# RWKV time mixing on one core: one batch a tile with contiguous runs, a fixed software pipeline, and transposes of bf16 pairs as float32 words

## The chip, the core and the metric

The kernel runs on one core of one Trainium2 chip. The metric is the device time of one execution in microseconds (us), taken as the median of several runs. A profile shows one execution, engine by engine: PE (TensorE, matmuls; its weight loads stand apart as PEld), DVE (VectorE), ACT (ScalarE), POOL (GpSimd) and SP (SyncE, which here only issues DMAs).

## What is computed

The input `x` holds 16 batches of 2048 tokens with 256 channels, in float32. Each token is mixed with the token before it in its batch (zeros ahead of the first), two projections follow, one passes a sigmoid, and their product goes through an output projection. The reference also computes `k`, which nothing uses; neither kernel computes it.

```python
x_prev[:, 1:, :] = x[:, :-1, :]
xv = x * time_mix_v + x_prev * (1 - time_mix_v)
xr = x * time_mix_r + x_prev * (1 - time_mix_r)
v = xv @ value_weight
r = xr @ receptance_weight
out = (sigmoid(r) * v) @ output_weight
```

## The kernel before

The work goes in 32 tiles of 1024 tokens (two a batch), and each tile in two halves of 512 tokens. Both kernels divide the mixing weight out: with c = 1/t - 1, the mixed value is t * (x + c * x_prev), and t is multiplied into the rows of the projection's weights once, at the start. So a mix is one multiplication (`x_prev` by c) and one addition.

For each tile POOL issues one DMA that loads 1024 rows of 1 KB and casts them to bf16 (L102, `x_bf`, 4 buffers). PE transposes it in 16 blocks of 128 x 128 bf16 into PSUM (L114), so that channels lie on the partitions, in two groups of 128 channels (`ko`), and tokens along the free dimension. ACT copies the two PSUM tiles into `xt` (L120, L121), one column to the right, so that column t holds token t - 1; column 0 is a memset or a copy of the last tile's last column (L124, L126). DVE makes `mix`: four multiplications of 128 x 1024 (L132) and two additions of 128 x 2048 (L141), one for v and one for r. For each half PE makes `psum_v` and `psum_r` (L151, L160, four matmuls of 512 columns each), ACT takes the sigmoid of `psum_r` into `s_sb` (L169), DVE multiplies it by `psum_v` into `z_sb` (L171), PE makes `psum_o` with eight matmuls of 256 columns whose stationary operand is `z_sb` (L176), and ACT copies it to `o_sb` in bf16 (L183). After both halves POOL issues one DMA that stores the tile and casts it to float32 (L185).

`psum_v`, `psum_r` and `psum_o` have one buffer each. The order on each engine is made by the scheduler of the Tile framework; within an engine instructions run in that order. All DMAs of `x` and `out` stand in the one queue of POOL.

Of the kernel before, what the change touches and what calls it, by code (L numbers as in the profile page):

```python
# [1 line left out]

# [6 lines left out]
FP32 = mybir.dt.float32  # L10
BF16 = mybir.dt.bfloat16
ALU = mybir.AluOpType
ACT = mybir.ActivationFunctionType


@with_exitstack
def kernel(
    ctx: ExitStack,
    tc: tile.TileContext,
    x: bass.AP,  # L20
    time_mix_k: bass.AP,
    time_mix_v: bass.AP,
    time_mix_r: bass.AP,
    key_weight: bass.AP,
    value_weight: bass.AP,
    receptance_weight: bass.AP,
    output_weight: bass.AP,
    out: bass.AP,
):
# [12 lines left out]

    ident = consts.tile([P, P], BF16)
    make_identity(nc, ident)

    tmv_sb = consts.tile([P, KO], FP32)
    nc.sync.dma_start(out=tmv_sb, in_=time_mix_v.rearrange("(ko p) -> p ko", p=P))
    tmr_sb = consts.tile([P, KO], FP32)
    nc.sync.dma_start(out=tmr_sb, in_=time_mix_r.rearrange("(ko p) -> p ko", p=P))

    cv_sb = consts.tile([P, KO], FP32)
    nc.vector.reciprocal(cv_sb, tmv_sb)
    nc.vector.tensor_scalar(  # L53
        out=cv_sb, in0=cv_sb, scalar1=-1.0, scalar2=None, op0=ALU.add
    )
    cr_sb = consts.tile([P, KO], FP32)
    nc.vector.reciprocal(cr_sb, tmr_sb)
    nc.vector.tensor_scalar(
        out=cr_sb, in0=cr_sb, scalar1=-1.0, scalar2=None, op0=ALU.add
    )  # L60
    c_sb = [cv_sb, cr_sb]

    ones = consts.tile([P, T], BF16)
    nc.vector.memset(ones, 1.0)
    c_full = []
    for m in range(2):
        cf = consts.tile([P, KO, T], BF16, name=f"c_full{m}")
        for ko in range(KO):
            nc.scalar.mul(out=cf[:, ko, :], in_=ones, mul=c_sb[m][:, ko : ko + 1])  # L69
        c_full.append(cf)  # L70

    wv_f32 = consts.tile([P, KO, D], FP32)
    nc.sync.dma_start(out=wv_f32, in_=value_weight.rearrange("(ko p) n -> p ko n", p=P))
    wr_f32 = consts.tile([P, KO, D], FP32)
    nc.sync.dma_start(
        out=wr_f32, in_=receptance_weight.rearrange("(ko p) n -> p ko n", p=P)
    )

    wv_bf = consts.tile([P, KO, D], BF16)
    wr_bf = consts.tile([P, KO, D], BF16)  # L80
    wo_bf = consts.tile([P, KO, D], BF16)
    for ko in range(KO):
        nc.scalar.mul(out=wv_bf[:, ko, :], in_=wv_f32[:, ko, :], mul=tmv_sb[:, ko : ko + 1])
        nc.scalar.mul(out=wr_bf[:, ko, :], in_=wr_f32[:, ko, :], mul=tmr_sb[:, ko : ko + 1])
    nc.gpsimd.dma_start(out=wo_bf, in_=output_weight.rearrange("(ko p) n -> p ko n", p=P))  # L85

    xpool = ctx.enter_context(tc.tile_pool(name="xpool", bufs=4))
    xtpool = ctx.enter_context(tc.tile_pool(name="xtpool", bufs=3))
    mixpool = ctx.enter_context(tc.tile_pool(name="mixpool", bufs=3))
    zpool = ctx.enter_context(tc.tile_pool(name="zpool", bufs=4))  # L90
    opool = ctx.enter_context(tc.tile_pool(name="opool", bufs=3))
    ps_xt_pool = ctx.enter_context(tc.tile_pool(name="ps_xt", bufs=2, space=bass.MemoryType.PSUM))
    ps_vr_pool = ctx.enter_context(tc.tile_pool(name="ps_vr", bufs=1, space=bass.MemoryType.PSUM))
    ps_o_pool = ctx.enter_context(tc.tile_pool(name="ps_o", bufs=1, space=bass.MemoryType.PSUM))

    prev_xt = None
    for b in range(B):
        for it in range(NT):
            t0 = it * T

            x_bf = xpool.tile([P, 2 * HB, D], BF16, name="x_bf")
            nc.gpsimd.dma_start(  # L102
                out=x_bf,
                in_=x[b, t0 : t0 + T, :].rearrange("(tb p) d -> p tb d", p=P),
            )

            xt = xtpool.tile([P, KO, XTW], BF16, name="xt")

            psum_xt = []
            for h in range(2):  # L110
                ps = ps_xt_pool.tile([P, KO, TH], BF16, name="ps_xt")
                for tb in range(HB):
                    for ko in range(KO):
                        nc.tensor.transpose(  # L114
                            out=ps[:, ko, tb * P : (tb + 1) * P],
                            in_=x_bf[:, h * HB + tb, ko * P : (ko + 1) * P],
                            identity=ident,
                        )
                psum_xt.append(ps)
            nc.scalar.copy(out=xt[:, :, 1 : 1 + TH], in_=psum_xt[0])  # L120
            nc.scalar.copy(out=xt[:, :, 1 + TH : 1 + T], in_=psum_xt[1])  # L121

            if it == 0:
                nc.vector.memset(xt[:, :, 0:1], 0.0)  # L124
            else:
                nc.vector.tensor_copy(out=xt[:, :, 0:1], in_=prev_xt[:, :, T : T + 1])  # L126
            prev_xt = xt

            mix = mixpool.tile([P, 2, KO, T], BF16, name="mix")
            for m in range(2):  # L130
                for ko in range(KO):
                    nc.vector.tensor_scalar(  # L132
                        out=mix[:, m, ko, :],
                        in0=xt[:, ko, 0:T],
                        scalar1=c_sb[m][:, ko : ko + 1],
                        scalar2=None,
                        op0=ALU.mult,
                    )
            xwin = xt[:, :, 1 : T + 1]
            for m in range(2):  # L140
                nc.vector.tensor_tensor(  # L141
                    out=mix[:, m], in0=mix[:, m], in1=xwin, op=ALU.add
                )

            o_sb = opool.tile([P, 2, HB, D], BF16, name="o_sb")
            for h in range(2):
                psum_v = ps_vr_pool.tile([P, KO, TH], FP32, name="psum_v")
                psum_r = ps_vr_pool.tile([P, KO, TH], FP32, name="psum_r")
                for mo in range(KO):
                    for ko in range(KO):  # L150
                        nc.tensor.matmul(  # L151
                            out=psum_v[:, mo, :],
                            lhsT=wv_bf[:, ko, mo * P : (mo + 1) * P],
                            rhs=mix[:, 0, ko, h * TH : (h + 1) * TH],
                            start=(ko == 0),
                            stop=(ko == KO - 1),
                        )
                for mo in range(KO):
                    for ko in range(KO):
                        nc.tensor.matmul(  # L160
                            out=psum_r[:, mo, :],
                            lhsT=wr_bf[:, ko, mo * P : (mo + 1) * P],
                            rhs=mix[:, 1, ko, h * TH : (h + 1) * TH],
                            start=(ko == 0),
                            stop=(ko == KO - 1),
                        )

                s_sb = zpool.tile([P, KO, TH], BF16, name="s_sb")
                nc.scalar.activation(out=s_sb, in_=psum_r, func=ACT.Sigmoid)  # L169
                z_sb = zpool.tile([P, KO, TH], BF16, name="z_sb")  # L170
                nc.vector.tensor_tensor(out=z_sb, in0=s_sb, in1=psum_v, op=ALU.mult)  # L171

                psum_o = ps_o_pool.tile([P, HB, D], FP32, name="psum_o")
                for j in range(HB):
                    for ko in range(KO):
                        nc.tensor.matmul(  # L176
                            out=psum_o[:, j, :],
                            lhsT=z_sb[:, ko, j :: HB],
                            rhs=wo_bf[:, ko, :],
                            start=(ko == 0),  # L180
                            stop=(ko == KO - 1),
                        )
                nc.scalar.copy(out=o_sb[:, h], in_=psum_o)  # L183

            nc.gpsimd.dma_start(  # L185
                out=out[b, t0 : t0 + T, :].rearrange("(h p j) d -> p h j d", p=P, j=HB),
                in_=o_sb,
            )


# [28 lines left out]
```

## Time and profile before

| what | value |
|---|---|
| median of 3 runs | 261.02 us (259.26 to 261.79) |
| span of the profiled execution | 258.6 us |
| PE busy | 208.8 us, 81% of the span |
| DVE busy | 205.3 us, 79% |
| ACT busy | 192.0 us, 74% |
| POOL busy | 53.0 us, 20% |
| HBM read and written | 34.34 MB and 33.55 MB |

The span runs from the first to the last instruction of the profiled execution. A line of a group gives the source line, the engine, the operation, output and inputs by name, the shape and the count, then busy time and the mean of one in ns, then the idle time of the engine just before these instructions and what ended it. A line of the timeline gives start and duration in us, then the same names; a merged line has the count behind an x, and idle time and its releaser in brackets. Durations of neighbours on one engine overlap by some tens of ns, so what an instruction costs its engine is read from start to start.

### The profile page before, as it was taken

What the parts mean: (1) busy time and instruction counts of PE and PEld (TensorE: products, weight loads), DVE (VectorE), ACT (ScalarE), POOL (GpSimd) and SP (SyncE); (2) the same over time, 40 slices, a digit from 0 to 9 for tenths busy, and PEclk for the clock granted to TensorE, in tenths of its full rate; (3) what the DMA queues carried; (4) which work ended last, traced back from release to release, by engine and by line L of the source; (5) the groups of instructions that cost most, each with busy time, mean ns of one, the idle gap of its engine ahead of it and who ended that gap; (6) DMA issues with size and microseconds to landing.
All of it is one profiled execution on the core that took longest, in us unless ns stands there. A gap on an engine that the chain in (4) does not pass through costs nothing.

```text
span 258.6 us, 3915 instructions
## 1 busy us (share of the span) xinstructions
PE 208.8 (81%) x1508; PEld 136.5 (53%) x1536; DVE 205.3 (79%) x293; ACT 192.0 (74%) x202; POOL 53.0 (20%) x71
## 2 busy tenths in 40 slices
PE   0288989888988889888889888988888987787860
PEld 0265655555666556565556655655555664354430
DVE  3087999888889888888888998888888899885330
ACT  6678979777777887877777788787777777645640
POOL 7031421222222211222222221112211111100111
PEclk9999999999999999999999999999999999999997
DMA  5999999999999999999999999999974343344444
GB/s 114 188 198 197 150 270 220 275 230 233 227 202 200 197 214 245 238 219 231 228 230 213 197 195 206 243 243 224 224 205 162 111 153 119 116 153 165 162 162 162
DMA packets 43362, 51.24 MB, mean 198 GB/s; under 512 B 1616, under 2 KB 35152, under 8 KB 43344
## 3 DMA queue, kind: packets, MB, share of 16 engines
q0 software_dynamic: 42256, 50.47, 89.3%
q1 hardware_dynamic: 1088, 0.53, 0.7%
q8 instruction: 12, 0.20, 0.3%
q14 instruction: 6, 0.05, 0.1%
HBM read 34.34 MB, written 33.55 MB: 263 GB/s over the span
## 4 chain that ended last, share of the span: by engine, by line
issue 67%; POOL 16%; PE 6%; DMA 4%; ACT 3%; POOLq 1%
POOL x_bf L102 8%; POOL out_dram L185 8%; DMA x_bf<-in_x_dram 4%; PE ps_xt L114 2%; PE psum_v L151 2%; PE psum_r L160 1%; PE psum_o L176 1%; ACT xt L120 1%; ACT s_sb L169 1%; ACT xt L121 1%; POOL wo_bf L85 0%; ACT o_sb L183 0%; POOLq L214 0%; POOLq L185 0%; POOLq L102 0%
## 5 line engine op out<-in xcount | busy, mean ns | idle before, releaser
L171 DVE TENSOR_TENSOR z_sb<-s_sb,psum_v 128x1024 bf16<-128x1024 bf16 x64 | 77.8, 1216 | 31.6 <-PE psum_v L151 28.3
L183 ACT CAST o_sb<-psum_o 128x1024 bf16<-128x1024 f32 x64 | 65.9, 1030 | 37.3 <-PE psum_o L176 37.3
L176 PE MATMUL psum_o<-wo_bf,z_sb 128*128 128x256 bf16 x512 | 67.3, 274 | 16.5 <-DVE z_sb L171 16.4
L169 ACT ACTIVATE s_sb<-psum_r 128x1024 bf16<-128x1024 f32 x64 | 66.0, 1032 | 17.5 <-PE psum_r L160 16.6
L141 DVE TENSOR_TENSOR mix<-mix,xt 128x2048 bf16<-128x2048 bf16 x64 | 77.7, 1218 | 0.0
L160 PE MATMUL psum_r<-mix,wr_bf 128*128 128x512 bf16 x244 | 65.2, 379 | 5.1 <-ACT s_sb L169 4.4
L176 PEld LDWEIGHTS <-z_sb 128*128 128x128 bf16 x512 | 52.1, 115 | 30.8 <-DVE z_sb L171 30.5
L151 PE MATMUL psum_v<-mix,wv_bf 128*128 128x512 bf16 x240 | 64.3, 382 | 0.7 <-issue 0.2
L114 PE MATMUL ps_xt<-ident,x_bf 128*128 128x128 bf16 x512 | 41.0, 228 | 20.5 <-DMA x_bf<-in_x_dram 12.0
L185 POOL DMA_DIRECT2D out_dram<-o_sb x32 | 22.6, 705 | 169.2 <-ACT o_sb L183 169.2
L114 PEld LDWEIGHTS <-x_bf 128*128 128x128 bf16 x512 | 35.6, 102 | 37.8 <-issue 15.4
L160 PEld LDWEIGHTS <-wr_bf 128*128 128x128 bf16 x256 | 25.1, 98 | 30.1 <-issue 0.7
L132 DVE TENSOR_SCALAR mix<-xt,cv_sb 128x1024 bf16<-128x1024 bf16 x64 | 28.7, 490 | 9.4 <-ACT xt L121 9.3
L120 ACT COPY xt<-ps_xt 128x1024 bf16<-128x1024 bf16 x32 | 32.7, 1021 | 3.7 <-PE ps_xt L114 3.7
L102 POOL DMA_DIRECT2D x_bf<-in_x_dram x32 | 29.0, 907 | 30.5 <-PE ps_xt L114 30.4
L151 PEld LDWEIGHTS <-wv_bf 128*128 128x128 bf16 x256 | 25.2, 99 | 16.1 <-issue 0.6
L121 ACT COPY xt<-ps_xt 128x1024 bf16<-128x1024 bf16 x32 | 33.1, 1034 | 0.0
L132 DVE TENSOR_SCALAR mix<-xt,cr_sb 128x1024 bf16<-128x1024 bf16 x64 | 28.5, 484 | 0.0
L126 DVE COPY xt<-xt 128x2 bf16<-128x2 bf16 x16 | 2.7, 169 | 1.2
L69 ACT ACTIVATE c_full<-ones,cv_sb 128x1024 bf16<-128x1024 bf16 x2 | 2.2, 1140 | 1.4 <-DVE cv_sb L53 1.4
L69 ACT ACTIVATE c_full<-ones,cr_sb 128x1024 bf16<-128x1024 bf16 x2 | 2.2, 1132 | 0.0
L69 ACT ACT_TABLE_LOAD x1 | 1.3, 1283 | 0.7 <-PEq L203 0.7
(16 smaller groups left out, 8.0 us busy)
## 6 DMA issues: line engine op xcount, KB each, us to landing
out_dram<-o_sb POOLq DMA_DIRECT2D x32, 1024.0 KB, 4.9
x_bf<-in_x_dram POOLq DMA_DIRECT2D x32, 512.0 KB, 7.2
wv_f<-in_value_weight_dram SPq DMA_DIRECT2D x1, 256.0 KB, 4.2
wr_f<-n_receptance_weight_dram SPq DMA_DIRECT2D x1, 256.0 KB, 4.3
wo_bf<-in_output_weight_dram POOLq DMA_DIRECT2D x1, 128.0 KB, 4.5
tmv_sb<-in_time_mix_v_dram SPq DMA_DIRECT2D x1, 1.0 KB, 2.1
tmr_sb<-in_time_mix_r_dram SPq DMA_DIRECT2D x1, 1.0 KB, 2.2
```

What stands on the lines that cost most here:

```text
L102: nc.gpsimd.dma_start(out=x_bf, in_=x[b, t0 : t0 + T, :].rearrange("(tb p) d -> p tb d", p=P),)
L114: nc.tensor.transpose(out=ps[:, ko, tb * P : (tb + 1) * P], in_=x_bf[:, h * HB + tb, ko * P : (ko + 1) * P], identity=ident,)
L121: nc.scalar.copy(out=xt[:, :, 1 + TH : 1 + T], in_=psum_xt[1])
L132: nc.vector.tensor_scalar(out=mix[:, m, ko, :], in0=xt[:, ko, 0:T], scalar1=c_sb[m][:, ko : ko + 1], scalar2=None, op0=ALU.mult,)
L141: nc.vector.tensor_tensor(out=mix[:, m], in0=mix[:, m], in1=xwin, op=ALU.add)
L151: nc.tensor.matmul(out=psum_v[:, mo, :], lhsT=wv_bf[:, ko, mo * P : (mo + 1) * P], rhs=mix[:, 0, ko, h * TH : (h + 1) * TH], start=(ko == ...
L160: nc.tensor.matmul(out=psum_r[:, mo, :], lhsT=wr_bf[:, ko, mo * P : (mo + 1) * P], rhs=mix[:, 1, ko, h * TH : (h + 1) * TH], start=(ko == ...
L169: nc.scalar.activation(out=s_sb, in_=psum_r, func=ACT.Sigmoid)
L171: nc.vector.tensor_tensor(out=z_sb, in0=s_sb, in1=psum_v, op=ALU.mult)
L176: nc.tensor.matmul(out=psum_o[:, j, :], lhsT=z_sb[:, ko, j :: HB], rhs=wo_bf[:, ko, :], start=(ko == 0), stop=(ko == KO - 1),)
L183: nc.scalar.copy(out=o_sb[:, h], in_=psum_o)
L185: nc.gpsimd.dma_start(out=out[b, t0 : t0 + T, :].rearrange("(h p j) d -> p h j d", p=P, j=HB), in_=o_sb,)
```

## The change

The kernel is written anew. Its unit is 512 tokens, 64 units in all, 4 to a batch.

- **Layout.** A tile is a whole batch. Partition p holds 16 tokens in a row (`"(p j) d -> p j d"`), 16 KB in one run. Slot j is the 128 tokens 16p + j. The token before a token of slot j stands in slot j - 1 of the same partition, so `x_prev` is `xt` 128 columns to the left; for slot 0 it is slot 15, one column to the right, which one DVE copy of 128 x 2 x 127 makes for each batch (L141 of the new kernel, "boundary copy" below).
- **Transposes.** A slot's 256 bf16 channels are read as 128 float32 words, and one transpose with a float32 identity moves 128 tokens (L121). Word c carries channels 2c and 2c + 1. ACT's copy from PSUM reads the words as bf16 with a step of two elements and writes the even and the odd channels apart (L139). The rows of the two projections' weights and of the mixing weights are loaded in the same order (`"(p ko) n -> p ko n"`).
- **Order.** The order is written out by hand (`tc.manual_schedule()`). In unit g PE makes r(g), v(g), the transposes of unit g + 7 and the output of unit g - 1. DVE makes two multiplications of a mixing piece (1024 tokens of one of the two mixes, so two units' share of one mix), z(g), and that piece's addition; pieces run three units ahead. The first units have transposes and mixing in other amounts.
- **Stores.** `o_sb` is float32 and SP issues the stores, 1 MB for each two units (L217), in smaller parts for the last batch. POOL issues only the loads, 2 MB of `x` each, two batches ahead of the transposes.
- **Start.** Batch 0 is loaded in four parts, the weights are scaled on DVE, `wo` is cast on POOL, and four multiplications of constants that nothing used (`c_full`) are gone.

```diff
-    TH = 512
-    T = 2 * TH
+    UJ = 4
+    TU = UJ * P
+    NU = B * UB
+    LOOK = 7
...
+    def transpose_slot(ps, b, j, jj):
+        nc.tensor.transpose(
+            out=ps[:, jj * P : (jj + 1) * P],
+            in_=x_bf[b][:, j, :].bitcast(FP32),
+            identity=ident,
+        )
+    def channels(ps):
+        return ps.bitcast(BF16).rearrange("p (c two) -> p two c", two=KO)
+    def transposes(g):
+        b, e = divmod(g, UB)
...
+        nc.scalar.copy(out=xt[b][:, :, c0 : c0 + TU], in_=channels(ps))
+        if e == UB - 1 and b > 0:
+            nc.vector.tensor_copy(
+                out=xt[b][:, :, 1:P], in_=xt[b][:, :, J * P : (J + 1) * P - 1]
+            )
...
+    def mixing_add(b, m, lo, hi):
+        nc.vector.tensor_tensor(
+            out=mix[b][:, m, :, lo:hi],
+            in0=mix[b][:, m, :, lo:hi],
+            in1=xt[b][:, :, lo + P : hi + P],
+            op=ALU.add,
+        )
...
+            nc.sync.dma_start(out=dst[:, a : a + 2 * UJ, :], in_=o_sb[b][:, a : a + 2 * UJ, :])
...
+            if e == 0 and b + 2 < B:
+                load(b + 2, [(0, J)])
...
+    START_T = [3, 4, 7, 9]
...
+    for g in range(NU):
+        ps_r = project(g, 0, ps_r_pool, "psum_r")
+        s_sb = zpool.tile([P, KO, TU], BF16, name="s_sb")
+        nc.scalar.activation(out=s_sb, in_=ps_r, func=ACT.Sigmoid)
+        ps_v = project(g, 1, ps_v_pool, "psum_v")
+        if g == 0:
...
+        took = take_pieces(g + 3, 1 if g > 8 else 2)
+        for piece in took:
+            mixing_scale(*piece)
+        z_sb = zpool.tile([P, KO, TU], BF16, name="z_sb")
+        nc.vector.tensor_tensor(out=z_sb, in0=s_sb, in1=ps_v, op=ALU.mult)
+        for piece in took:
+            mixing_add(*piece)
+        advance(START_T[g] if g < len(START_T) else g + LOOK)
+        if z_prev is not None:
+            output(g - 1, z_prev)
+        z_prev = z_sb
+    output(NU - 1, z_prev)
```

The order of instructions moves at three places. The first is DVE in the middle of the program; before, one tile reads so (two products `z_sb`, four multiplications by the two constants `cv_sb` and `cr_sb`, two additions):

```order
L171 TENSOR_TENSOR z_sb<-s_sb,psum_v 128x1024
L132 TENSOR_SCALAR mix<-xt,cv_sb 128x1024 x2
L132 TENSOR_SCALAR mix<-xt,cr_sb 128x1024 x2
L141 TENSOR_TENSOR mix<-mix,xt 128x2048
L171 TENSOR_TENSOR z_sb<-s_sb,psum_v 128x1024
L141 TENSOR_TENSOR mix<-mix,xt 128x2048
```

In the changed kernel two units, with the boundary copy between them, read so:

```order
L292 TENSOR_TENSOR z_sb<-s_sb,psum_v 128x1024
L163 TENSOR_TENSOR mix<-mix,xt 128x2x1024
L141 COPY xt<-xt 128x2x127
L154 TENSOR_SCALAR mix<-xt,c_sb 128x1024 x2
L292 TENSOR_TENSOR z_sb<-s_sb,psum_v 128x1024
L163 TENSOR_TENSOR mix<-mix,xt 128x2x1024
```

The work between one `z_sb` and the next was one addition in one half and four multiplications with one addition in the other; now it is two multiplications and one addition each time.

The second place is PE's order around an output projection, with one weight load and matmul of each run shown. Before:

```order
L176 LDWEIGHTS z_sb
L176 MATMUL psum_o<-wo_bf,z_sb 128x256
...
L151 LDWEIGHTS wv_bf
L151 MATMUL psum_v<-mix,wv_bf 128x512
...
L160 LDWEIGHTS wr_bf
L160 MATMUL psum_r<-mix,wr_bf 128x512
...
L114 LDWEIGHTS x_bf
L114 MATMUL ps_xt<-ident,x_bf 128x128
```

In the changed kernel:

```order
L178 LDWEIGHTS w_bf
L178 MATMUL psum_r<-mix,w_bf 128x512
...
L178 LDWEIGHTS w_bf
L178 MATMUL psum_v<-mix,w_bf 128x512
L121 MATMUL ps_t<-ident,x_bf 128x128 x4
L194 LDWEIGHTS z_sb
L194 MATMUL psum_o<-wo_bf,z_sb 128x256
```

Before, the output projection of a half stood directly ahead of the next half's v; now v of unit g stands ahead of the output of unit g - 1, and four transposes, which have no weight load of their own in the program, stand between them.

The third place is POOL's queue at the start (`ident` is the identity of the transposes). Before:

```order
masks.py:197 MEMSET ident 128x128
L85 DMA wo_bf<-in_output_weight_dram 128x2x256
masks.py:199 ISA
masks.py:199 AFFINE_SELECT ident<-ident 128x128
L102 DMA x_bf<-in_x_dram 128x8x256 x9
L185 DMA out_dram<-o_sb 128x2x1024
```

In the changed kernel:

```order
L72 DMA x_bf<-in_x_dram 128x256
L80 DMA x_bf<-in_x_dram 128x1024
masks.py:197 MEMSET ident 128x128
masks.py:199 ISA
masks.py:199 AFFINE_SELECT ident<-ident 128x128
L80 DMA x_bf<-in_x_dram 128x1024
L80 DMA x_bf<-in_x_dram 128x1792
L118 CAST wo_bf<-wo_f_103 128x512
L72 DMA x_bf<-in_x_dram 128x4096 x2
```

The first loads are smaller and stand ahead of everything else; from there on POOL's queue holds loads and the memsets of the zero column, and no load stands behind a store.

More of the change, by code (lines that the diff above doesn't have):

```diff
@@ L79 @@
[L79 to L94, printed above, removed]
@@ new lines, in t_unit, with transposes0 @@
+    def t_unit(g):
+        b, e = divmod(g, UB)
+        if e == 0 and b + 1 < B and b + 1 not in x_bf:
+            load(b + 1, [(0, J)])
+        if g == 0:
+            return
+        transposes(g)
+    load(1, [(0, J)])
+    first_prev()
+    def transposes0(g):
+        ps = ps_t_pool.tile([P, TU], FP32, name="ps_t")
+        for jj in range(UJ):
+            transpose_slot(ps, 0, g * UJ + jj, jj)
+        c0 = (1 + g * UJ) * P
+        nc.scalar.copy(out=xt[0][:, :, c0 : c0 + TU], in_=channels(ps))
```

265 lines of the change are left out of this document (156 added, 109 removed).

## The prediction

> **What bounds the kernel now.** I read the page's busy times first, then the groups by line, then the timeline of one steady tile on DVE and on PE, then DMA in half-microsecond windows, then the two ends. The page says that no engine is full:
>
> ```profile
> PE 208.8 (81%) x1508; PEld 136.5 (53%) x1536; DVE 205.3 (79%) x293; ACT 192.0 (74%) x202; POOL 53.0 (20%) x71
> L171 DVE TENSOR_TENSOR z_sb<-s_sb,psum_v 128x1024 bf16<-128x1024 bf16 x64 | 77.8, 1216 | 31.6 <-PE psum_v L151 28.3
> L183 ACT CAST o_sb<-psum_o 128x1024 bf16<-128x1024 f32 x64 | 65.9, 1030 | 37.3 <-PE psum_o L176 37.3
> L176 PE MATMUL psum_o<-wo_bf,z_sb 128*128 128x256 bf16 x512 | 67.3, 274 | 16.5 <-DVE z_sb L171 16.4
> L121 ACT COPY xt<-ps_xt 128x1024 bf16<-128x1024 bf16 x32 | 33.1, 1034 | 0.0
> ```
>
> DVE's one large idle time is ahead of z, waiting for `psum_v`; PE's is ahead of `psum_o`, waiting for z. The timelines show how the two waits hang together, DVE first, then PE:
>
> ```profile
> 95.83 1.21 DVE L171 TENSOR_TENSOR z_sb<-s_sb,psum_v 128x1024 bf16<-128x1024 bf16 x1
> 96.96 1.22 DVE L141 TENSOR_TENSOR mix<-mix,xt 128x2048 bf16<-128x2048 bf16 x1
> 98.28 0.17 DVE L126 COPY xt<-xt 128x2 bf16<-128x2 bf16 x1
> 99.13 1.22 DVE L171 TENSOR_TENSOR z_sb<-s_sb,psum_v 128x1024 bf16<-128x1024 bf16 x1 [0.68 <-PE psum_v L151]
> 100.27 0.88 DVE L132 TENSOR_SCALAR mix<-xt,cv_sb 128x1024 bf16<-128x1024 bf16 x2
> 101.06 0.88 DVE L132 TENSOR_SCALAR mix<-xt,cr_sb 128x1024 bf16<-128x1024 bf16 x2
> 101.85 1.22 DVE L141 TENSOR_TENSOR mix<-mix,xt 128x2048 bf16<-128x2048 bf16 x1
> 102.99 1.21 DVE L171 TENSOR_TENSOR z_sb<-s_sb,psum_v 128x1024 bf16<-128x1024 bf16 x1
> 104.12 1.22 DVE L141 TENSOR_TENSOR mix<-mix,xt 128x2048 bf16<-128x2048 bf16 x1
> ```
>
> ```profile
> 97.09 1.06 PE L176 MATMUL psum_o<-wo_bf,z_sb 128*128 128x256 bf16 x8 [0.43 <-DVE z_sb L171]
> 98.00 1.03 PE L151 MATMUL psum_v<-mix,wv_bf 128*128 128x512 bf16 x4
> 98.86 1.03 PE L160 MATMUL psum_r<-mix,wr_bf 128*128 128x512 bf16 x4
> 103.05 0.78 PE L114 MATMUL ps_xt<-ident,x_bf 128*128 128x128 bf16 x11
> ```
>
> ```profile
> L114 PE MATMUL ps_xt<-ident,x_bf x16: 216/219/219, 100.2 to 103.6; 128*128 128x128 bf16 x16
> ```
>
> The first z ends at 97.04, the output projection starts at 97.09, the next v behind it runs from 98.00 to 99.03, and the next z starts at 99.13. So one half costs a round trip DVE to PE and back, 99.13 - 95.83 = 3.30 us, though DVE has only z, an addition and a small copy to do in it. In the other half, 102.99 - 99.13 = 3.86 us, DVE is the bound: z, four multiplications, an addition. A tile is 7.16 us, 3.58 a unit of 512 tokens.
>
> From start to start z costs DVE 1.14 us, an addition 1.14, two multiplications 0.79: 3.07 a unit (tile: 6.14 of 7.16). PE's terms: psum_v 0.86, psum_r the same, psum_o 0.91, a bf16 transpose (0.78 - 0.22) / 10 = 0.056 (0.22 is the length of the last one itself, the median of the row above). DMA is not the bound:
>
> ```profile
> 104.00:104.50 0.50, 0.24 (x2) 0.25 (x3) 0.50 (x2) 0.34 (x1) 0.37 (x1) 1.00 0.13 49
> 104.50:105.00 0.50, 0.50 (x7) 0.50 (x6) 0.50 (x1) 0.00 (x0) 0.50 (x1) 1.00 1.28 451
> 109.50:110.00 0.50, 0.50 (x4) 0.20 (x2) 0.50 (x1) 0.50 (x1) 0.00 (x0) 1.00 1.31 177
> 110.50:111.00 0.50, 0.49 (x9) 0.32 (x6) 0.50 (x1) 0.50 (x1) 0.50 (x1) 1.00 0.09 12
> ```
>
> The last two columns are DMA share and GB/s, bytes counted as they land. Store (float32, 451) and load (bf16, 177, so 354 of float32 read) each fill the queue, from 104.5 on, and at 110.5 both are through: about 5.7 us of work in a tile of 7.16, or 2.85 a unit.
>
> **The change part by part.** *The steady unit.* z(g), which v(g+1) needs for its PSUM buffer, now runs while PE does transposes, the last output and r(g+1), so the round trip is covered: v(g) to v(g+1) on PE leaves 0.91 + 0.86 us and the transposes between them, z takes 1.21. Mixing is spread evenly, two multiplications and one addition a unit. DVE then needs 1.14 + 1.14 + 0.79 = 3.07 us. New is the boundary copy, 15 in all, 254 elements. Bounds: the 0.17 above for 4 elements, and 0.44 for 1024 (half of an 0.88 pair); I take 0.3 (it starts a column off, and the odd length may cost it the fast rate), 0.08 a unit: **3.15**.
>
> *PE.* 0.86 + 0.86 + 0.91 = 2.63, and four float32 transposes at t each. No row has a float32 matmul. The nearest:
>
> ```profile
> L114 PE MATMUL ps_xt<-ident,x_bf 128*128 128x128 bf16 x512 | 41.0, 228 | 20.5 <-DMA x_bf<-in_x_dram 12.0
> L114 PEld LDWEIGHTS <-x_bf 128*128 128x128 bf16 x512 | 35.6, 102 | 37.8 <-issue 15.4
> ```
>
> From below t is 0.056, if a word costs what a bf16 element costs; from above it is 4 x (0.102 + 0.056) = 0.63, if the engine, all of whose rows here have 16-bit operands, splits both float32 operands into two halves and makes 2 x 2 transposes, each with its weight load bare. I take 0.10, one weight load not hidden, since data is only moved and the words are twice as wide: PE 3.03, just under DVE. On this two rules of the Trainium skill pull apart. FP8 and Floating Point Precision, TensorE Precision Notes, says that true float32 takes four passes; by it alone t would be 0.22 or more and PE the bound, a rival below. TensorE: Matmul & The Clock Gate, Terms, says that on trn2 the transpose mode is four times faster for FP32, which gives 0.056 and leaves the sum. No run here shows either.
>
> *ACT.*
>
> ```profile
> 100.01 1.04 ACT L169 ACTIVATE s_sb<-psum_r 128x1024 bf16<-128x1024 f32 x1
> 100.93 1.04 ACT L121 COPY xt<-ps_xt 128x1024 bf16<-128x1024 bf16 x1
> 101.82 1.05 ACT L183 CAST o_sb<-psum_o 128x1024 bf16<-128x1024 f32 x1
> ```
>
> Three instructions a unit, 0.91 from start to start: 2.73. Two things are new: float32 output, which I price at nothing because the element count sets these rows (bf16 or float32 input, 1.03 both), and the step of two in the read of PSUM, from nothing to double, 0.91. I take nothing; there are 0.42 us of cover under DVE.
>
> *DMA.* The same bytes cross HBM. Runs grow from 1 KB to 16 KB on the load and 4 KB to 8 KB on the store, and SP takes the stores. I price both at the old 2.85 a unit, which fits under 3.15; better is likely, and worth nothing while DVE is the bound. Loads stand two batches ahead (some 25 us), so waits of POOL's queue are covered; its own memset stands behind them and waits for additions that are one unit past.
>
> *The start and the end.*
>
> ```profile
> 10.45 1.89 PE L114 MATMUL ps_xt<-ident,x_bf 128*128 128x128 bf16 x16 [10.45 <-DMA x_bf<-in_x_dram]
> 2.46 3.53 POOL L102 DMA_DIRECT2D x_bf<-in_x_dram  x4
> 2.23 0.48 SPq L75 DMA_DIRECT2D wr_f<-n_receptance_weight_dram  x1
> 21.83 1.22 DVE L171 TENSOR_TENSOR z_sb<-s_sb,psum_v 128x1024 bf16<-128x1024 bf16 x1 [1.10 <-ACT s_sb L169]
> wr_f<-n_receptance_weight_dram SPq DMA_DIRECT2D x1, 256.0 KB, 4.3
> L83 ACT ACTIVATE wv_bf<-wv_f,tmv_sb 128x256 bf16<-128x256 f32 x2 | 1.0, 492 | 0.0
> ```
>
> Before, the first x landed at 10.45 behind four loads and wo, and the first z ran at 21.83. Now the first transposes need 0.5 MB of float32 issued 2 us earlier, and DVE does not wait for 1024 tokens. I put weights there at 6.5 (second one issued at 2.2, 4.3 to land), four scalings of at most 0.49 to 7.2, unit 0's mixing of half size to 9.8, eight matmuls of 0.43 behind the first of two additions to 12.6 (twice 0.216: the first 16 transposes above take 1.89, half the later pace), and the first z at **13.0**, an estimate.
>
> From there DVE has 64 z x 1.14 = 73.0, 62 pieces x (1.14 + 0.79) = 119.7 and 15 copies x 0.3 = 4.5: **197.2**. It idles in the ramp, where nothing runs ahead yet. Walking the first six units through the written order with these durations I get three waits: the multiplications behind z(0) wait for two copies of ACT behind it (1.6), z(2) for an r and a v that waited for additions behind z(1) (1.1), the first boundary copy for three copies of ACT (2.0): **4.6**. At the end mixing is out at unit 60, and PE's 2.63 a unit against z's 1.14 makes DVE idle 3 x 1.5 = **4.4**; before, these units went at the round trip of 3.3. Behind the last z:
>
> ```profile
> 249.28 1.22 DVE L171 TENSOR_TENSOR z_sb<-s_sb,psum_v 128x1024 bf16<-128x1024 bf16 x1 [2.09 <-PE psum_v L151]
> 250.55 1.06 PE L176 MATMUL psum_o<-wo_bf,z_sb 128*128 128x256 bf16 x8 [1.38 <-DVE z_sb L171]
> 251.66 1.01 ACT L183 CAST o_sb<-psum_o 128x1024 bf16<-128x1024 f32 x1 [2.30 <-PE psum_o L176]
> 252.96 0.71 POOL L185 DMA_DIRECT2D out_dram<-o_sb  x1 [5.92 <-ACT o_sb L183]
> ```
>
> From 250.50 to 258.6 is 8.1 us; now the copy is halved over two engines and 0.25 MB go out in place of 1 MB, with a cheaper issue: **5.1**, from 1.1 + 0.6 + 0.4 and some 3 to land (SP's small weights took 4.3 beside other traffic).
>
> Sum: 13.0 + 197.2 + 4.6 + 4.4 + 5.1 = 224.3 us of span. The profiled run's span was 258.6 where the median is 261.02, 2.4 more: **227 us**.
>
> **The rivals.** (1) *PE becomes the bound, 2 x 2 transposes at the bf16 pace*: t = 0.22, PE 3.51, and 51 steady units with transposes lose 0.36 each, 18: 245. For it: wide data, and no float32 row against it. (2) *The same with bare weight loads, slower than before*: t = 0.63, PE 5.15 a unit in the same four instructions, 51 x 2.0 = 102: 329. It decides from t = 0.30, where 34 / 51 = 0.67 a unit eats the gain. For it: the transposes stand in the program as one instruction with no separate weight load, so nothing shows that the load runs ahead. Against it: bf16 loads of 0.102 hide fully at a pace of 0.056, and a transpose only moves data. (3) *ACT's step of two*: 2.73 + 0.91 = 3.64, 51 x 0.49 = 25: 252. The Trainium skill, PSUM — Partial Sum Buffer, Specifications, gives PSUM 8-byte lines that make non-contiguous patterns slow for matmuls; no run here shows what ACT does. Against it: both halves of each 8-byte line are still read. (4) *DMA*: loads and stores now mix in two queues; if the mixture runs no faster than the old tile took, 3.58 a unit, 58 x 0.43 = 25: 252. Against it: 2.85 was the queue's full time. (5) *The change does not do what it says*: some buffer's wait puts the round trip back in each unit, 3.58 again, and only the ends gain, against added copies: about 260.
>
> **How the numbers follow.** 227 has 0.60, rival 1 0.13, rival 2 0.09, rival 3 0.06, rival 4 0.07, rival 5 0.05. The likeliest case alone spans 219 (start and boundary copy at their low bounds, no ramp idle) to 235 (hand-offs of 0.1 us a unit between nearly equal engines). The range goes to 250 and takes in rival 1 and what is halfway to 3 and 4; 329 is left out. Faster by over 1% (about what a measurement of this kernel can tell from no change): 0.60 + 0.13 + 0.06 + 0.07 = 0.86; within 1%: 0.05; slower: 0.09.
>
> **What would show it.** Right: DVE near 90% busy with no wait for `psum_v` in the middle, z starts 3.1 to 3.2 us apart, the first z at 12 to 14, PE's wait ahead of `psum_o` gone. t is read from starts of neighbouring transposes: wrong at 0.13 or more, where PE's 2.63 + 4t passes 3.15. ACT's copy at 1.03 us acquits the step of two. Waits for `x_bf` on PE past unit 8 would make DMA the bound.

## The result and the profile after

The changed kernel takes 228.56 us (median of 4 runs, 228.05 to 228.9), the kernel before 260.73 us beside it (4 runs). The ratio is 0.877, with a 95% interval of 0.873 to 0.880, so 32 us are gone. The profiled execution has a span of 226.3 us. Its page, busy times first, then the chain that ended last, then the groups that answer to those shown of before:

```profile
PE 201.0 (89%) x1260; PEld 130.1 (58%) x1281; DVE 203.4 (90%) x288; ACT 185.3 (82%) x194; POOL 13.1 (6%) x41
...
DVE 76%; issue 9%; PE 6%; ACT 3%; DMA 3%; POOL 1%; POOLq 0%; DVEq 0%
...
L292 DVE TENSOR_TENSOR z_sb<-s_sb,psum_v 128x1024 bf16<-128x1024 bf16 x64 | 77.6, 1213 | 4.8 <-ACT s_sb L281 2.9
L139 ACT COPY xt<-ps_t 128x1024 bf16<-128x1024 bf16 x60 | 60.4, 1013 | 18.0 <-PE ps_t L121 17.9
L212 ACT COPY o_sb<-psum_o 128x1024 f32<-128x1024 f32 x63 | 64.2, 1018 | 6.8 <-PE psum_o L194 6.8
L194 PE MATMUL psum_o<-wo_bf,z_sb 128*128 128x256 bf16 x512 | 66.4, 273 | 1.1 <-ACT o_sb L212 1.1
L121 PE MATMUL ps_t<-ident,x_bf 128*128 128x128 f32 x257 | 39.3, 279 | 11.6 <-DMA x_bf<-in_x_dram 11.0
L121 PEld LDWEIGHTS ps_t<-ident,x_bf 128*128 128x128 f32 x257 | 32.1, 143 | 24.0 <-issue 8.6
```

DVE's busy time has hardly moved (203.4 us after 205.3); the span has come down towards it. The two large waits of before are gone: ahead of z 4.8 us are left of 31.6, ahead of `psum_o` 1.1 of 16.5. The chain that ended last is now DVE for 76%. The middle of the run in one row (window, length, then busy time and instructions of PE, PEld, DVE, ACT, POOL, then clock, DMA share, GB/s):

```profile
40.00:200.00 160.00, 156.63 (x1003) 103.33 (x1020) 158.72 (x218) 145.18 (x153) 6.58 (x22) 1.00 0.84 241
```

DVE works 158.72 of 160 us there. Two units of the timeline, DVE and PE together:

```profile
110.86 1.21 DVE L292 TENSOR_TENSOR z_sb<-s_sb,psum_v 128x1024 bf16<-128x1024 bf16 x1
111.24 1.03 PE L178 MATMUL psum_r<-mix,w_bf 128*128 128x512 bf16 x4
111.99 1.22 DVE L163 TENSOR_TENSOR mix<-mix,xt 128x2048 bf16<-128x2048 bf16 x1
112.13 1.02 PE L178 MATMUL psum_v<-mix,w_bf 128*128 128x512 bf16 x4
112.99 0.60 PE L121 MATMUL ps_t<-ident,x_bf 128*128 128x128 f32 x4
113.13 0.22 DVE L141 COPY xt<-xt 128x254 bf16<-128x254 bf16 x1
...
113.42 1.04 PE L194 MATMUL psum_o<-wo_bf,z_sb 128*128 128x256 bf16 x8
113.45 0.89 DVE L154 TENSOR_SCALAR mix<-xt,c_sb 128x1024 bf16<-128x1024 bf16 x2
114.26 1.21 DVE L292 TENSOR_TENSOR z_sb<-s_sb,psum_v 128x1024 bf16<-128x1024 bf16 x1
...
115.52 1.02 PE L178 MATMUL psum_v<-mix,w_bf 128*128 128x512 bf16 x4 [0.20 <-DVE z_sb L292]
...
117.31 1.21 DVE L292 TENSOR_TENSOR z_sb<-s_sb,psum_v 128x1024 bf16<-128x1024 bf16 x1
```

From z to z are 3.05 us without a boundary copy (114.26 to 117.31) and 3.40 with one, and none of DVE's rows waits. `psum_v` is complete at 113.15, 1.1 us before the z at 114.26 reads it. The output of the z that ended at 112.07 starts at 113.42, and no v stands close behind it: r and the next v follow, and the z that this v waits for is another one. That wait is left, but it is short: the copy delays the z at 114.26, v at 115.52 waits 0.20 us for it (4.6 us for all such waits of the run, 17 of them) and is still complete 0.8 us ahead of the next z. So what z makes has more than a microsecond to reach PE, and before it had to be there at once.

By stage, the 32.3 us of span came from three places. Up to the start of the ninth z, with the ramp behind, 4.8 us are won (48.04 after 52.85; the first z has 6.2). From there to the last z it is 171.1 us after 196.4 (48.04 to 219.15, 52.85 to 249.28), 25.3 us for 55 units or 0.46 each. Behind the last z's end there are 5.9 us after 8.1, 2.2.

### The profile page after: what moved, and what is told of

It reads as the page before. It is cut to its first block, busy times and chain, and to the rows that moved or that the text cites. A ratio compares the mean times of both kernels' runs of the same rounds, so it can differ in the third digit from the quotient of the medians.

```text
span 226.3 us, 3393 instructions
## 1 busy us (share of the span) xinstructions
PE 201.0 (89%) x1260; PEld 130.1 (58%) x1281; DVE 203.4 (90%) x288; ACT 185.3 (82%) x194; POOL 13.1 (6%) x41
## 4 chain that ended last, share of the span: by engine, by line
DVE 76%; issue 9%; PE 6%; ACT 3%; DMA 3%; POOL 1%; POOLq 0%; DVEq 0%
DVE mix L163 31%; DVE z_sb L292 30%; DVE mix L154 15%; DMA x_bf<-in_x_dram 3%; PE psum_v L178 2%; PE psum_o L194 2%; PE psum_r L178 2%; ACT xt L235 1%; ACT xt L139 1%; DVE xt L141 1%; PE ps_t L121 1%; POOL xt L134 1%; ACT o_sb L212 0%; DVE o_sb L209 0%; ACT o_sb L207 0%
## 5 line engine op out<-in xcount | busy, mean ns | idle before, releaser
L178 PEld LDWEIGHTS <-w_bf 128*128 128x128 bf16 x512 | 49.8, 98 | 59.5 <-issue 11.8
L163 DVE TENSOR_TENSOR mix<-mix,xt 128x2048 bf16<-128x2048 bf16 (+1 forms) x66 | 77.8, 1184 | 0.0
L139 ACT COPY xt<-ps_t 128x1024 bf16<-128x1024 bf16 x60 | 60.4, 1013 | 18.0 <-PE ps_t L121 17.9
L178 PE MATMUL psum_v<-mix,w_bf 128*128 128x512 bf16 x255 | 66.1, 380 | 5.1 <-DVE z_sb L292 4.6
L212 ACT COPY o_sb<-psum_o 128x1024 f32<-128x1024 f32 x63 | 64.2, 1018 | 6.8 <-PE psum_o L194 6.8
L178 PE MATMUL psum_r<-mix,w_bf 128*128 128x512 bf16 x236 | 65.2, 383 | 3.0 <-DVE mix L163 2.0
L154 DVE TENSOR_SCALAR mix<-xt,c_sb 128x1024 bf16<-128x1024 bf16 (+1 forms) x132 | 56.4, 472 | 3.8 <-ACT xt L235 2.2
L121 PE MATMUL ps_t<-ident,x_bf 128*128 128x128 f32 x257 | 39.3, 279 | 11.6 <-DMA x_bf<-in_x_dram 11.0
L121 PEld LDWEIGHTS ps_t<-ident,x_bf 128*128 128x128 f32 x257 | 32.1, 143 | 24.0 <-issue 8.6
L72 POOL DMA_DIRECT2D x_bf<-in_x_dram x16 | 8.6, 539 | 122.7 <-PE ps_t L121 121.9
L235 ACT COPY xt<-ps_t 128x1024 bf16<-128x1024 bf16 x4 | 4.0, 1014 | 9.4 <-PE ps_t L121 9.4
L141 DVE COPY xt<-xt 128x254 bf16<-128x254 bf16 x15 | 3.3, 218 | 2.0 <-ACT xt L139 2.0
L80 POOL DMA_DIRECT2D x_bf<-in_x_dram x3 | 1.6, 542 | 0.0
## 6 DMA issues: line engine op xcount, KB each, us to landing
x_bf<-in_x_dram POOLq DMA_DIRECT2D x15, 1024.0 KB, 10.2
```

Source lines behind the costliest of these rows:

```text
L72: nc.gpsimd.dma_start(out=x_bf[b][:, lo:hi, :], in_=src[:, lo:hi, :])
L121: nc.tensor.transpose(out=ps[:, jj * P : (jj + 1) * P], in_=x_bf[b][:, j, :].bitcast(FP32), identity=ident,)
L139: nc.scalar.copy(out=xt[b][:, :, c0 : c0 + TU], in_=channels(ps))
L141: nc.vector.tensor_copy(out=xt[b][:, :, 1:P], in_=xt[b][:, :, J * P : (J + 1) * P - 1])
L154: nc.vector.tensor_scalar(out=mix[b][:, m, ko, lo:hi], in0=xt[b][:, ko, lo:hi], scalar1=c_sb[:, m, ko : ko + 1], scalar2=None, op0=ALU.mult,)
L163: nc.vector.tensor_tensor(out=mix[b][:, m, :, lo:hi], in0=mix[b][:, m, :, lo:hi], in1=xt[b][:, :, lo + P : hi + P], op=ALU.add,)
```

## The experiments

All are edits of the changed kernel, each timed beside the kernel before; 0.877 is the ratio to keep in mind. The theory is that the time comes from the order alone: the output made one unit late covers the round trip of z, and the even mixing uses the time. The rivals are that the layout and its long transfers, the stores on SP, or the transposes bring it, or that the gain at the start is what counts.

### The order: output ahead of v

```diff
         nc.scalar.activation(out=s_sb, in_=ps_r, func=ACT.Sigmoid)
+        if z_prev is not None:
+            output(g - 1, z_prev)
         ps_v = project(g, 1, ps_v_pool, "psum_v")
...
         advance(START_T[g] if g < len(START_T) else g + LOOK)
-        if z_prev is not None:
-            output(g - 1, z_prev)
         z_prev = z_sb
```

> The output of unit g - 1 is put ahead of v(g) again; all else is as in the changed kernel. Order theory (the gain is the covered round trip; DVE at 3.14 us a unit is the bound now): each z waits again for z, output, v in a row, 3.30 us a unit, so 0.16 to 0.2 us a unit more and 2 us at the end, 238 to 241 us, with DVE waiting for psum_v before most z. Rival (the gain comes from longer runs, stores on SP and fewer transposes, and the engines were slowed by DMA before): the order matters little, 228 to 231.

Measured: 242.86 us, ratio 0.931 (0.928 to 0.934), 1.9 us above the range. Timeline of this kernel:

```profile
111.76 1.22 DVE L294 TENSOR_TENSOR z_sb<-s_sb,psum_v 128x1024 bf16<-128x1024 bf16 x1
113.04 1.05 PE L194 MATMUL psum_o<-wo_bf,z_sb 128*128 128x256 bf16 x8
113.92 1.03 PE L178 MATMUL psum_v<-mix,w_bf 128*128 128x512 bf16 x4
115.06 1.22 DVE L294 TENSOR_TENSOR z_sb<-s_sb,psum_v 128x1024 bf16<-128x1024 bf16 x1
118.35 1.22 DVE L294 TENSOR_TENSOR z_sb<-s_sb,psum_v 128x1024 bf16<-128x1024 bf16 x1
```

The round trip of 3.30 us is back, to the hundredth: z ends at 112.98, `psum_o` starts at 113.04, v behind it ends at 114.95, the next z starts at 115.06. It now holds in every unit without a boundary copy, since DVE's even 3.06 is less; with the copy DVE itself needs 3.40. A batch takes 13.28 us (three of 3.29 or 3.30, and 3.40) after 12.57, which makes 9.3 us from the ninth z to the 61st. The rest of the 14.8 us between the two profiled spans is in the ramp, 3.9 (the third z comes at 26.77 in place of 24.19), and at the end, where the last z are 3.30 apart in place of 2.4 to 2.8; behind the last z 0.5 is won back.

### The order: mixing as unevenly as before

```diff
-        took = take_pieces(g + 3, 1 if g > 8 else 2)
+        if g <= 8:
+            took = take_pieces(g + 3, 2)
+        elif g % 2 == 1:
+            took = take_pieces(g + 4, 2)
+        else:
+            took = []
         for piece in took:
             mixing_scale(*piece)
+        if g > 8 and took:
+            mixing_add(*took[0])
+            took = took[1:]
```

> From unit 9 on, mixing is taken in the pattern of before: both pieces of two units between two z (four multiplications, one addition), the second addition behind the next z. The output stays behind v. Order theory: DVE never runs dry, because the v of the next unit has a whole unit's time, so 228 to 232 us; evenness by itself is worth little. If evenness is what matters: 3.58 a unit as before, 250 or more. Rival of data movement: 228 to 230.

Measured: 238.03 us, ratio 0.911 (0.907 to 0.916): a miss, since I had taken it for free. The z of one batch:

```profile
143.16 1.22 DVE L300 TENSOR_TENSOR z_sb<-s_sb,psum_v 128x1024 bf16<-128x1024 bf16 x1
147.60 1.22 DVE L300 TENSOR_TENSOR z_sb<-s_sb,psum_v 128x1024 bf16<-128x1024 bf16 x1
150.00 1.22 DVE L300 TENSOR_TENSOR z_sb<-s_sb,psum_v 128x1024 bf16<-128x1024 bf16 x1
153.85 1.21 DVE L300 TENSOR_TENSOR z_sb<-s_sb,psum_v 128x1024 bf16<-128x1024 bf16 x1
156.29 1.22 DVE L300 TENSOR_TENSOR z_sb<-s_sb,psum_v 128x1024 bf16<-128x1024 bf16 x1
```

The short half, in which DVE has z and one addition (2.27 us), takes 2.40 and 2.44. A shorter round trip is left there, z to v to z: elsewhere in this run a z starts at 121.35, v waits 0.65 us for it and runs from 122.62 to 123.64, and the next z starts at 123.75, 2.40 us. The long half takes 3.85, and 4.44 with the copy: 0.33 of that is the copy's own, and the rest lies ahead of it, where DVE waits for ACT's copy of the same unit's transposes (it ends at 118.25, the boundary copy starts at 118.28), which the even mixing did not wait for. A batch is 13.13 us where the changed kernel has 12.57; about half of the difference is the two short halves, the other half this wait. In the profiled runs the last z comes 10.8 us later: 0.9 of it before the edit sets in (the ninth z at 48.91), 1.9 at the unit where the pattern begins with two pieces at once (5.31 us to the next z, 3.39 in the changed kernel), and 8.0 behind it, of which some 12.5 batches at 0.56 make 7.

### The order: both

The two edits above in one kernel:

```diff
+        if z_prev is not None:
+            output(g - 1, z_prev)
         ps_v = project(g, 1, ps_v_pool, "psum_v")
...
+        elif g % 2 == 1:
+            took = take_pieces(g + 4, 2)
```

> Both at once: output ahead of v, and uneven mixing. Layout, long runs, stores on SP and float32 transposes stay. Order theory: one half bound by the round trip at 3.30, the other by DVE at 3.86 and a quarter of 0.34 for the boundary copy a unit, so some 3.6 a unit, 255 to 262 us, nearly all of the gain gone. Rival of data movement: most of the gain stays, under 240.

Measured: 264.91 us, ratio 1.015 (1.010 to 1.020), 2.9 us above the range. This decides between the theory and the layout, the stores and the transposes, all of which stay. The waits of this kernel (waiting instruction, releaser, us in total, times, longest):

```profile
PEld L194 <- DVE z_sb L302: 62.3, 59, 2.6
DVE z_sb L302 <- PE psum_v L178: 33.9, 31, 3.1
PE psum_o L194 <- DVE z_sb L302: 30.1, 32, 2.1
```

They are the two waits of the kernel before, z for `psum_v` (28.3 us there, 33.9 here) and `psum_o` for z (16.4 there, 30.1 here). The z start at 109.22, 112.51, 116.98, 120.27 and 124.12: 3.29, 4.47 with the copy, 3.29, 3.85. A batch takes 14.90 us, the two tiles of before 14.32. The spans add up with that: from the ninth z to the last this kernel takes 8.2 us more than the one before, 14 batches at 0.58, and it wins 0.8 up to the ninth z and 2.6 behind the last, so that its span is 4.8 us longer (263.4 after 258.6). All of the 0.58 is in the half with the boundary copy (4.47 for 3.85): 0.33 is the copy's own, and the rest again its wait for ACT. Without the order, the boundary copies cost more than everything else in the change brings.

Of the 36 us between this kernel and the changed one, the late output brings 27 where the mixing stays uneven, and the even mixing 22 where the output stays early.

### The transposes: bf16 in place of float32 words

```diff
-        nc.tensor.transpose(
-            out=ps[:, jj * P : (jj + 1) * P],
-            in_=x_bf[b][:, j, :].bitcast(FP32),
-            identity=ident,
-        )
+        for ko in range(KO):
+            nc.tensor.transpose(
+                out=ps[:, ko, jj * P : (jj + 1) * P],
+                in_=x_bf[b][:, j, ko * P : (ko + 1) * P],
+                identity=ident,
+            )
```

`ident`, `ps_t` and the order of the weights' rows follow.

> Only the transposes go back: eight of bf16 a unit in place of four of float32, plain channel order in weights and PSUM, ACT's copy with step one. Order theory: eight at 0.056 us are 0.45, four at 0.11 are 0.44, and ACT's copy costs 1.01 either way, so no change: 227 to 230 us. If halving the transposes is part of the gain: 233 or more.

Measured: 229.0 us, ratio 0.877 (0.874 to 0.881), no difference. PE's rows say why; this kernel's eight transposes, and what follows them:

```profile
110.72 0.61 PE L122 MATMUL ps_t<-ident,x_bf 128*128 128x128 bf16 x8
111.16 1.04 PE L195 MATMUL psum_o<-wo_bf,z_sb 128*128 128x256 bf16 x8
```

Eight cost PE 0.44 us here, four float32 ones 0.43 in the changed kernel (112.99 to 113.42). The pairing halves the instructions and saves no time. ACT's copy, here with step one, takes 1.013 us, as with the step of two.

### The transposes: each made twice

```diff
-        for jj in range(UJ):
-            transpose_slot(ps, b, e * UJ + jj, jj)
+        for rep in range(2):
+            for jj in range(UJ):
+                transpose_slot(ps, b, e * UJ + jj, jj)
```

> From batch 1 on each transpose is made twice, with the same result (batch 0 as before). This loads PE by four more float32 transposes a unit, 0.44 us. Theory that PE stands just under DVE (3.07 against 3.14 a unit): PE becomes the bound at 3.5 a unit, 53 units lose 0.37, so 246 to 250 us. Rival (PE has room, its busy share overstates): under 236.

Measured: 246.19 us, ratio 0.944 (0.940 to 0.949). The page and a steady unit:

```profile
PE 225.3 (92%) x1494; PEld 157.6 (64%) x1521; DVE 208.0 (85%) x288; ACT 185.5 (76%) x194; POOL 13.0 (5%) x41
...
L293 DVE TENSOR_TENSOR z_sb<-s_sb,psum_v 128x1024 bf16<-128x1024 bf16 x64 | 78.1, 1220 | 17.5 <-ACT s_sb L282 15.3
```

```profile
109.32 1.04 PE L121 MATMUL ps_t<-ident,x_bf 128*128 128x128 f32 x8
110.20 1.04 PE L195 MATMUL psum_o<-wo_bf,z_sb 128*128 128x256 bf16 x8
113.67 1.04 PE L195 MATMUL psum_o<-wo_bf,z_sb 128*128 128x256 bf16 x8
```

The second four cost their full 0.44 us, PE's unit is 3.47, and PE bounds the kernel. This is rival 1 of the prediction built by hand (3.51 a unit, 245 us), so its price was right and its condition not met. It also shows how little room PE has.

### The transfers: 1 KB rows

```diff
-        src = x[b].rearrange("(p j) d -> p j d", p=P)
+        src = x[b].rearrange("(j p) d -> p j d", p=P)
...
-        dst = out[b].rearrange("(p j) d -> p j d", p=P)
+        dst = out[b].rearrange("(j p) d -> p j d", p=P)
```

> Loads and stores go by 1 KB rows again: a slot is 128 tokens in a row in HBM. This leaves out the right previous token (slots are then 128 tokens apart), with the same instructions and bytes. Order theory: DMA work is 2.85 us a unit or a little more, under DVE's 3.14, so 228 to 233 us, the start perhaps a little later. Rival of data movement: the gain hangs on the long runs, 240 or more, with PE waiting for x_bf.

Measured: 229.22 us, ratio 0.879 (0.874 to 0.884), within the error of the changed kernel. The middle of this kernel:

```profile
40.00:200.00 160.00, 156.22 (x1002) 103.03 (x1018) 158.72 (x217) 145.17 (x153) 12.71 (x22) 1.00 1.11 243
```

The DMA share rises from 0.84 to 1.11 and a load takes 15.8 us to land in place of 10.2, but DVE is busy for the same 158.72 us. The long runs make the DMA engines' work cheaper, and nothing waits for it.

### The stores on POOL

```diff
-            o_sb[b] = opool.tile([P, J, D], FP32, name="o_sb")
+            o_sb[b] = opool.tile([P, J, D], BF16, name="o_sb")
...
-                nc.sync.dma_start(out=dst[:, a : a + 2, :], in_=o_sb[b][:, a : a + 2, :])
+                nc.gpsimd.dma_start(out=dst[:, a : a + 2, :], in_=o_sb[b][:, a : a + 2, :])
```

The two other stores alike.

> Stores go back to POOL's queue with the cast from bf16; everything else stays. Order theory: loads stand two batches ahead, and a store in front of a load waits for ACT at most two units, so 228 to 231 us, the end 1 us longer at most. Rival of data movement: stores block loads, 235 or more, with PE waiting for x_bf.

Measured: 232.34 us, ratio 0.891 (0.886 to 0.895), 1.3 us above the range. The middle is unchanged (DVE 158.72 of 160 again). The end:

```profile
220.95 1.22 DVE L292 TENSOR_TENSOR z_sb<-s_sb,psum_v 128x1024 bf16<-128x1024 bf16 x1 [1.38 <-ACT s_sb L281]
...
224.59 0.53 POOL L210 DMA_DIRECT2D out_dram<-o_sb  x1 [1.18 <-ACT o_sb L207]
225.31 0.53 POOL L210 DMA_DIRECT2D out_dram<-o_sb  x1 [0.20 <-issue]
```

The span ends at 231.1, 8.9 us behind the last z and not 5.9; another 1.8 are lost in the ramp (the fourth z at 31.14 in place of 29.36). SP's queue and float32 stores are worth 4 us, all at the ends.

### The boundary copy on POOL

```diff
-            nc.vector.tensor_copy(
+            nc.gpsimd.tensor_copy(
                 out=xt[b][:, :, 1:P], in_=xt[b][:, :, J * P : (J + 1) * P - 1]
```

> The boundary copy goes from DVE to POOL, 15 x 0.33 us less on DVE. Theory that DVE's own work is the bound: 4 us less at best, since PE's 3.07 a unit comes next, so 224 to 226 us if POOL's copy ends before the multiplications behind it; if POOL needs over 0.8 us for it or blocks DVE, 228 to 230. Rival (DVE is not the bound): 228 to 229 with DVE idle by as much.

Measured: 224.38 us, ratio 0.860 (0.855 to 0.865). Timeline of this kernel around one copy:

```profile
109.46 1.21 DVE L292 TENSOR_TENSOR z_sb<-s_sb,psum_v 128x1024 bf16<-128x1024 bf16 x1
110.23 0.39 POOL L141 COPY xt<-xt 128x254 bf16<-128x254 bf16 x1 [10.22 <-ACT xt L139]
112.52 1.21 DVE L292 TENSOR_TENSOR z_sb<-s_sb,psum_v 128x1024 bf16<-128x1024 bf16 x1
115.58 1.21 DVE L292 TENSOR_TENSOR z_sb<-s_sb,psum_v 128x1024 bf16<-128x1024 bf16 x1
```

Taking 15 times 0.33 us, 5 us, from DVE brings 4.2 us: DVE sets the pace. The 13 copies behind the ninth z bring theirs in full (4.3 us from there to the last z); the two in the ramp bring nothing, since the multiplications behind them wait for POOL's copy and start later than before (27.97 and 38.32 after 27.77 and 38.07). In the middle DVE is now busy for 160.00 of 160 us.

### The start: a late part of the first load

```diff
     load0(4, 8)
-    load0(8, 15)
...
     nc.gpsimd.tensor_copy(out=wo_bf, in_=wo_f32)
+    load0(8, 15)
```

> The load of the last seven slots of batch 0 (0.9 MB of float32) moves behind the cast of wo on POOL, so it no longer runs beside the first loads and the weights; nothing else changes. Theory that the first z came 2.6 us later than forecast (15.6 for 13.0) because the first load shares a full DMA with everything issued in the first 3 us: the first transposes of unit 0 start at 6.5 to 7.3 in place of 8.2, the first z at 14 to 15, and the median is 227 to 228. Rival (latency of the first load, not sharing): first transposes stay at 8.2 and the median at 228.6, or later where units 2 and 3 wait for the moved part.

Measured: 228.43 us (6 runs), ratio 0.875 (0.872 to 0.877). The first transposes of unit 0 start at 7.98 in place of 8.20, the first z at 15.65 in place of 15.59. In this form the theory of the start fell: a load of 448 KB out of the way brings the first transposes forward by 0.2 us, and the first z not at all.

### The start: late part and copy on POOL together

```diff
-    load0(8, 15)
...
+    load0(8, 15)
...
-            nc.vector.tensor_copy(
+            nc.gpsimd.tensor_copy(
```

> The boundary copy on POOL and the late load together. If both gains stand and add up: 222.5 to 224. If the start's gain is lost in the ramp's waits behind it: 224 to 225, as with the copy alone.

Measured: 224.25 us, ratio 0.859 (0.856 to 0.862), the copy's gain alone.

### The start: only what the first unit needs

On top of the copy on POOL, nothing but the first two parts of `x`, the two projections' weights and the mixing weights (1 KB each) is loaded in the first 5 us. POOL waits for the first weights with a tiny copy, and loads the rest of batch 0 and `wo` behind it.

```diff
     load0(0, 4)
     make_identity(nc, ident)
-    load0(4, 8)
-    load0(8, 15)
...
-    wo_f32 = consts.tile([P, KO, D], FP32)
-    nc.sync.dma_start(out=wo_f32, in_=output_weight.rearrange("(ko p) n -> p ko n", p=P))
+    gate = consts.tile([P, 1], FP32)
+    nc.gpsimd.tensor_copy(out=gate, in_=w_f32[:, 0, 0, 0:1])
+    load0(4, 8)
...
-    nc.gpsimd.tensor_copy(out=wo_bf, in_=wo_f32)
+    load0(8, 15)
+    nc.gpsimd.dma_start(out=wo_bf, in_=output_weight.rearrange("(ko p) n -> p ko n", p=P))
```

> On top of the boundary copy on POOL: in the first 5 us only the first two loads of x and the two projections' weights are under way; POOL waits for the first weights, then issues the other parts of batch 0 and the load of wo (with the cast, so the cast on POOL is gone), then batches 1 and 2. Theory that what shares the DMA in the first 8 us sets the first transposes (1.9 MB land by 8.0 with the late part alone, here 1.2 MB are ahead of unit 0): first transposes of unit 0 at 6.3 to 6.8, first z at 14 or a little before, 222.5 to 223.5 us. Rival (it is set by the latency of that one load, or by the order on DVE): first transposes at 7.5 or later, 224 to 224.5.

Measured: 222.92 us (6 runs), ratio 0.854 (0.851 to 0.857), the best of all. Its start:

```profile
6.89 1.12 PE L121 MATMUL ps_t<-ident,x_bf 128*128 128x128 f32 x4 [2.06 <-DMA x_bf<-in_x_dram]
7.04 0.61 DVE L110 TENSOR_SCALAR w_bf<-w_f,tms 128x256 bf16<-128x256 f32 x2 [1.48 <-DMA w_f<-in_value_weight_dram]
...
10.89 1.86 PE L178 MATMUL psum_r<-mix,w_bf 128*128 128x512 bf16 x4
...
14.57 1.22 DVE L292 TENSOR_TENSOR z_sb<-s_sb,psum_v 128x1024 bf16<-128x1024 bf16 x1
```

The time came out as expected; the first transposes came 0.1 and the first z 0.6 us later than expected. With less issued beside it, the load that unit 0 needs is there 1.3 us sooner (8.20 to 6.89), and 1.0 of it reaches the first z. Which of the loads that were put off does it is not shown; the 448 KB alone brought 0.2.

## Why the prediction was right, and where it was not

The forecast was 227 us and the mechanism is the one it named: DVE bounds the steady unit, since the round trip is covered. The terms, in us:

| term | forecast | measured |
|---|---|---|
| steady unit on DVE | 3.15 | 3.14: three of 3.06 and one of 3.40, by 4 |
| a float32 transpose, t | 0.10 | 0.11: 0.43 by 4 |
| PE's unit | 3.03 | 3.06 at DVE's pace; 3.03 from the doubled transposes (3.47 less 0.44) |
| first z | 13.0 | 15.59 |
| DVE's work to the end of the last z | 197.2 | 197.5: 204.8 less the waits |
| waits in the ramp | 4.6 | 4.3: 1.10 + 1.20 + 2.02 |
| waits at the end | 4.4 | 2.9: 1.55 + 1.38 |
| behind the last z | 5.1 | 5.9 |
| outside the span | 2.4 | 2.3 |

The sum is 228.5. Two terms came out more than half a microsecond longer than forecast (the first z 2.6, behind the last z 0.8) and one shorter (the waits at the end, 1.5). These offset each other in part, so that a total within 2 us of the forecast is partly luck; the steady unit, which makes up most of the time, is not.

**The first z.** Forecast were the weights at 6.5, the last scaling done at 7.2, unit 0's mixing directly behind it and done at 9.8. The changed kernel's rows:

```profile
8.20 1.12 PE L121 MATMUL ps_t<-ident,x_bf 128*128 128x128 f32 x4 [3.44 <-DMA x_bf<-in_x_dram]
8.36 0.61 DVE L111 TENSOR_SCALAR w_bf<-w_f,tms 128x256 bf16<-128x256 f32 x2 [2.84 <-DMA w_f<-in_value_weight_dram]
9.36 1.01 ACT L235 COPY xt<-ps_t 128x1024 bf16<-128x1024 bf16 x1 [7.34 <-PE ps_t L121]
10.40 1.16 DVE L154 TENSOR_SCALAR mix<-xt,c_sb 128x512 bf16<-128x512 bf16 x4 [1.09 <-ACT xt L235]
12.21 1.86 PE L178 MATMUL psum_r<-mix,w_bf 128*128 128x512 bf16 x4 [0.68 <-DVE mix L163]
```

The step that failed is the arrival of `x`: the forecast gave it no time of its own and let the scalings set the start. Unit 0's part of `x`, issued at 1.89, is there at 8.20; with the transposes and ACT's copy behind it the mixing starts at 10.40, 3.2 us late, and is done at 12.76. The weights were late too: the second took 6.2 us to land and not the 4.3 of the row from before, so that the scaling ended at 8.97. But DVE waits 1.09 us more behind it, for ACT's copy, so the weights did not set the first z. The kernel with 1 KB rows shows the same: there all scalings are done at 6.49, the first transposes start at 8.15 all the same, and the first z at 16.23. The last experiment, where the transposes start 1.3 us sooner, has its z 1.0 sooner. The first matmuls at half pace, 1.86 us for four, were forecast as such.

**The waits at the end** were taken as three of 1.5; there were two, the first of 1.55 at the last z but one, since the last addition (212.51) still stands between the third and the fourth z from the end.

**Behind the last z** there are 0.8 us more, from two waits that the forecast did not have:

```profile
220.84 1.03 PE L194 MATMUL psum_o<-wo_bf,z_sb 128*128 128x256 bf16 x8 [1.10 <-ACT o_sb L212]
221.91 0.59 ACT L207 COPY o_sb<-psum_o 128x512 f32<-128x512 f32 x1 [1.12 <-PE psum_o L194]
222.53 0.69 DVE L209 COPY o_sb<-psum_o 128x512 f32<-128x512 f32 x1 [2.16 <-ACT o_sb L207]
```

The last output starts 0.47 us behind the end of z (220.37), because its PSUM buffer is still being copied by ACT. And the two halves of the last copy, meant for two engines at once, run one behind the other, 0.6 us more. The landing, forecast at some 3, gives a little back.

**The rivals.** Rivals 1 and 2 fall with t: four passes would be 0.22, and PE would bound from 0.13. The Trainium skill pulled two ways here: FP8 and Floating Point Precision, TensorE Precision Notes, would have true float32 take four passes; TensorE: Matmul & The Clock Gate, Terms, has the transpose mode four times faster for FP32. The trace agrees with neither as I had worked them out: 0.11 is twice the cost of a bf16 transpose, not four times and not once. Rival 3 falls with ACT's copy, 1.013 us with a step of two in PSUM, and 1.013 dense in the kernel with bf16 transposes (1.034 before); the Trainium skill's rule in PSUM — Partial Sum Buffer, Specifications, that non-contiguous patterns are slow, speaks of matmuls and does not show in this read by ACT. Rival 4 (DMA) falls with a share of 0.84 and with the 1 KB rows. Rival 5 did not come, and the first three experiments show that its price was too high for its condition: with the round trip back in each unit 18 of the 32 us are left, and only with uneven mixing besides none.

One thing the forecast had right for an incomplete reason: it counted the even mixing as a matter of DVE's sum alone. The uneven kernel shows that it matters beyond this, since a half with little work in it is shorter than the round trip that is left, z to v to z, and since the boundary copy then comes too early and waits for ACT.

## What to carry to other kernels

Where no engine is full and two engines wait for each other in turn, write down the round trip of one unit from the timeline and compare it with the busiest engine's work between its ends; the larger of the two is the time, and this holds unit by unit, not on the mean. Delay the consumer by one unit, then spread the other work evenly so that no unit is shorter than the round trip that is left. Expect changes of layout, run length or instruction count on resources that nothing waits for to bring nothing, and try each of them alone before they are given the credit.

## What the runs showed of the hardware

- A float32 transpose of 128 x 128 costs PE 0.11 us from start to start, its weight load has rows of 0.143 us; a bf16 one 0.056 and 0.10. Per byte moved they are equal.
- ACT reads bf16 from PSUM with a step of two as fast as densely, 1.013 us each for 1024 elements a partition.
- Runs of 1 KB and of 8 to 16 KB move the same bytes in the same kernel time here (243 and 241 GB/s in the middle), but with a DMA share of 1.11 against 0.84, and a load takes 15.8 us to land against 10.2.
- The boundary copy costs DVE 0.33 us with its gaps for 254 elements, and POOL 0.39 us in 14 of the 15 cases; the one that ran beside two of DVE's additions took 1.68 us (1.68 and 1.69 in the two other kernels with the copy on POOL).
